# Four sequence mixers on one core: another rule for the order of the instructions, chains with buffers of their own, and transposes in a later step

## The chip, the cores and the metric

The kernel runs on one core of one Trainium2 chip. The metric is the device time of one execution in microseconds (us); lower is better. TensorE is called PE here, VectorE DVE, ScalarE ACT, GpSimd POOL and SyncE SP, as the profile does.

## The reference

The input x has 2048 tokens of 1024 features. One layer computes, in float32:

```python
h = _rmsnorm(x, pre_norm_w[l])
proj = jnp.einsum('btd,de->bte', h, w_in[l])
p_gdn, p_rwkv, p_sc, p_gla = _split(proj, [GDN_COLS, RWKV_COLS, SC_COLS, GLA_COLS])
...
y = jnp.concatenate([y_gdn, y_rwkv, y_sc, y_gla], axis=-1)
out = jnp.einsum('bte,ed->btd', y, w_out[l])
x = x + _rmsnorm(out, post_norm_w[l])
```

Each of the four mixers makes 256 of the 1024 features of y. Gated-delta (gdn) works in chunks of 64 tokens with 4 heads of 64: per chunk and head a lower triangular 64x64 matrix has to be inverted, and then a state of 64x64 goes from chunk to chunk:

```python
v_new = u_c - jnp.einsum('bhck,bhkv->bhcv', w_c, s)
o = jnp.einsum('bhck,bhkv->bhcv', q_c, s) + jnp.einsum('bhij,bhjv->bhiv', attn_c, v_new)
s = s * jnp.exp(gl_c)[..., None, None] + jnp.einsum('bhck,bhcv->bhkv', k_c, v_new)
```

RWKV-7 is written in the reference as one step per token; the kernel brings it into the same form (a triangular inverse per chunk and a state passed on). The short convolution (sc) has no state, and gated linear attention (gla) has a state but no inverse.

## The kernel before, in words

The 2048 tokens are cut into 4 blocks of 512 (`NBLK`, `BL`), a block into 4 tiles of 128 tokens (`TT`), a tile into 2 chunks. Per block there is much dense work on PE: the input projection, 760 matmuls of 512 columns that write the PSUM tiles called `pp` (`proj`, L476; each weight is used as a high and a low part, with the high and low part `hh`, `hl` of the normalised input). After the blocks the output projection has 768 more of them (`out_proj`, `woh` and `wol`), partly begun earlier; 3808 in all.

Beside it stand chains of small matmuls, which wait for DVE or ACT at nearly each step:

- the inverse (`inverse`, L558), once for two tiles, 16 times in all: steps on PE that write `psi`, eight matmuls each, in turn `psi<-X,Bb` (its result goes through DVE into `W`, L591) and `psi<-W,Yb` (through DVE into `X`, L596, and its transpose `Y`, L598, copied into `Yb`, L583);
- the chains of gdn (`gdn_chain`) and rwkv (`rwkv_chain`), in chunks one after the other: steps that write `psc`. One chunk of rwkv is `psc<-Sr,AR`, then an ACT copy into `ru` (L1034), `psc<-ru,Yf`, then DVE into `UV` (L1042), `psc<-UV,BKT`, then DVE into the state `Sr` (L1015);
- the preparation (`gdn_mats`, `rwkv_mats`, `gates_prep`, `rwkv_prep`), whose matmuls and transposes write `psa`.

What sets the order. First the program is recorded by generators (`chains`, `inverses`, `prepare`, `put`, `stats`, `projections`), which `weave` steps in turn on a clock of its own: it counts PE's time by the formulas in `mm` and `tr`, and a chain that yields a latency from the table `LAT` is taken up again when that much PE work has been recorded. `self.done` and a yielded tuple are events: ("B", n) is matrices n recorded, ("I", n) inverse n recorded, ("G", blk) and ("R", blk) the chain of a block. Then, when the `TileContext` closes (opened at L1431), its scheduler orders the recorded instructions of each engine by their priority and by its own clock of when operands, buffers and engines are ready, and puts in the semaphores. On the chip each engine takes its instructions in that order.

Buffers are rings (`RINGS`, `RINGS_G`, `RINGS16`): so many tiles of a name, used in turn. The part of the preparation for inverse n (`prepare`, L1110 on) waits for ("I", n - 1), since `Bh` and `Bl` have one buffer each.

Of the kernel before, what the change touches and what calls it, by code (L numbers as in the profile page):

```python
# [19 lines left out]
P = 128  # L20
# [105 lines left out]
class Ring:  # L126
# [6 lines left out]
    def __call__(self):  # L133
# [10 lines left out]

    "M4": (512, 4), "BKT": (512, 2), "UV": (512, 2), 
    "ru": (256, 2), "lu": (256, 3), "or": (256, 2),  "Yf": (64 * 8, 1), "y": (256, 1),
    "t2": (BL, 4), "gk": (16, 9), "sx": (64, 1), "dr": (16, 1), "kn": (4 * TT, 3), "rB": (256, 1), "sm": (16, 14),

# [5 lines left out]
RINGS_G = {  # L154
    "kq": (2 * BL, 2), "gv": (BL, 2), "ggz": (2 * BL, 1), "attn": (256, 2), "kT": (256, 4), "vT": (256, 2),
    "gu": (256, 3), "t1": (256, 3), "og": (256, 2), "gy": (256, 1),
}
RINGS16 = {"Bh": 1, "Bl": 1, "W": 1, "X": 2, "Y": 1}
RINGSBD = {"Bb": 1, "Yb": 2}
# [10 lines left out]

LAT = {"gates": 6.0, "ipre": 2.0, "gates2": 1.0, "norms": 3.2, "chan": 0.9, "pool": 1.38, "decay": 2.6, "mats": 2.2, "inv0": 1.0, "inv1": 2.2,
       "invr": 0.8, "chA": 1.0, "chB": 0.7, "chC": 0.48, "rpre": 5.0, "rchan": 4.5, "gpre": 3.0, "gA": 1.1,
# [15 lines left out]
class K:  # L188
# [581 lines left out]
    def gdn_mats(self, tt, Bh, Bl):  # L770
# [9 lines left out]
        nc.vector.tensor_tensor(h4(mb), m4(self.incl), bc(g["kb"]), ALU.mult)  # L780
        kT, vT = g["kT"][tt], self.R["vT"]()
        nc.vector.tensor_tensor(h4(kT), h4(kT), bc(g["ke"]), ALU.mult)
        ps = self.psa()
        for pr in range(2):
            self.tr(ps[:, pr * P:(pr + 1) * P], g["v"][pr][:, tt * P:(tt + 1) * P], self.ident)
        nc.vector.tensor_tensor(h4(vT), h4(ps[:, 0:256]), bc(g["kv"]), ALU.mult)
        yield LAT["pool"]
# [19 lines left out]
        nc.gpsimd.tensor_tensor(Bl, h4(B32), Bh, ALU.subtract)  # L807
        return dict(attn=h4(attn), kT=kT, vT=vT)

# [37 lines left out]
    def rwkv_prep(self, blk):  # L847
# [10 lines left out]
        for pr in range(2):  # L858
# [16 lines left out]
            ev = e.rearrange("p (a c) t -> p a c t", c=2)  # L875
            en, ak = self.t2(), self.t2()
            nc.scalar.activation(en, G, AF.Exp, scale=-1.0)
            kk = self.t2()
            nc.scalar.activation(m3(kk), k_, AF.Copy, scale=self.d[:, 23 + pr:24 + pr])
# [47 lines left out]
    def rwkv_mats(self, tt, Bh, Bl):  # L927
# [21 lines left out]
        nc.gpsimd.tensor_tensor(Bl, h4(B32), Bh, ALU.subtract)  # L949
        for pr in range(2):  # L950
            bd = BK[pr][:, 2 * tt:2 * tt + 2, :]
            for c in range(2):
                nc.scalar.activation(bd[:, c], bd[:, c], AF.Copy, scale=r["dec"][:, pr, 2 * tt + c:2 * tt + c + 1])
        yield LAT["rdec"]
        ps = self.psa()
        for cp in range(2):
            for pr in range(2):
                o = (2 * cp + pr) * P
                self.tr(ps[:, o:o + P], BK[pr][:, 2 * tt + cp, :], self.ident)
        bt = self.R["BKT"]()  # L960
        nc.scalar.copy(bt, ps)
        ps = self.psa()
# [3 lines left out]
        for cp in range(2):  # L966
            nc.scalar.copy(uv[hs(1 - cp), cp, :], ps[hs(cp), 0:256])
        return dict(M4=M4, bt=bt, uv=uv)

# [47 lines left out]
    def rwkv_chain(self, tt, m, Y):  # L1017
# [11 lines left out]
        for cp in range(2):  # L1029
# [80 lines left out]
    def prepare(self):  # L1110

        n = 0
        for blk in range(NBLK):
            for name in "GR":
                if name == "G":
                    yield "P", blk, "gdn"
                    yield from self.gates_prep()
                    yield from self.gdn_prep()
                else:
                    yield "P", blk, "rwkv"  # L1120
                    yield from self.rwkv_prep(blk)
                    self.done("Rprep", blk)
                for pair in range(TT // 2):
                    if n:
                        yield "I", n - 1
                    B, ms = [self.R16[x]() for x in ("Bh", "Bl")], []
                    for i in range(2):
                        if pair:
                            yield "T", name, blk, i
                        m = yield from (self.gdn_mats if name == "G" else self.rwkv_mats)(2 * pair + i, *(t[:, 4 * i:4 * i + 4, :] for t in B))  # L1130
                        ms.append(m)
                    self.mats[n] = ms, B
                    self.done("B", n, lat=LAT["mats"])
# [301 lines left out]
```

## Time and profile before

| | |
|---|---|
| time of 3 runs | 1380.93 us median (1374.62 to 1382.09) |
| profiled execution | 1382.66 us, span 1380.9 us |
| PE busy | 1286.0 us, 93% of the span |
| DVE, ACT, POOL busy | 966.9, 532.1 and 357.1 us |
| granted PE clock | 0.979 of full speed on average |
| DMA engines | 44.6% of their span |

A PE matmul's row covers its way through the array, so that rows that follow each other overlap; the pace is read from start to start. A row's bracket says how long the engine was idle before it, and what it waited for. DVE, ACT and POOL rows are the time of one instruction.

### The profile page before, as it was taken

To read this page: it belongs to the slowest core of one execution; us is meant where nothing else is said; L and a number is where in the kernel's file an instruction comes from. 1 tells how busy PE (TensorE), PEld (TensorE's weight loads), DVE (VectorE), ACT (ScalarE), POOL (GpSimd) and SP (SyncE) were. 2 spreads that over 40 slices of the span, in tenths; PEclk is the share of its full clock that TensorE was granted. 3 is DMA by queue.
4 is the path that set the end of the run, shared out by engine and by line. 5 is a ranking of instruction groups with operands and counts; after the bars stand their busy time and mean duration, and the time that the engine had idled before them with its cause. 6 is when DMAs were issued, how large, how long until landed. Compare 5 with 4: busy or idle time off the path is not lost. (4 is left out here: it accounts for less than half of the span.)

```text
span 1380.9 us, 25696 instructions
## 1 busy us (share of the span) xinstructions
PE 1286.0 (93%) x9928; PEld 974.5 (71%) x9928; DVE 966.9 (70%) x2194; ACT 532.1 (39%) x1165; POOL 357.1 (26%) x437
## 2 busy tenths in 40 slices
PE   5989988899999999999999899999998998999997
PEld 3767766667767777767677677676776776777886
DVE  5776697778886787688757894888669847643222
ACT  4653454235442441435524422453234234232221
POOL 5564443301121121111311211103112144232221
PEclk9999999999999999999999999999999998999999
DMA  7876554453244424453444333532444362233442
GB/s 278 272 253 228 206 176 145 142 167 121 92 139 136 155 93 151 140 177 123 139 145 137 123 126 130 165 125 93 146 134 142 117 213 87 93 111 100 150 151 99
DMA packets 98506, 204.47 MB, mean 148 GB/s; under 512 B 9152, under 2 KB 39248, under 8 KB 98384
## 3 DMA queue, kind: packets, MB, share of 16 engines
q1 hardware_dynamic: 98384, 202.83, 44.6%
q8 instruction: 78, 1.28, 0.4%
q14 instruction: 44, 0.36, 0.1%
HBM read 153.51 MB, written 49.28 MB: 147 GB/s over the span
## 5 line engine op out<-in xcount | busy, mean ns | idle before, releaser
L197 PE MATMUL pp<-hh,w 128*128 128x512 f32 (+1 forms) x2272 | 642.2, 408 | 7.9 <-ACT hh L432 4.0
L197 PEld LDWEIGHTS pp<-hh,w 128*128 128x128 f32 (+1 forms) x2272 | 413.0, 190 | 96.8 <-issue 5.1
L197 PE MATMUL pp<-hl,w 128*128 128x512 f32 (+1 forms) x1152 | 340.7, 408 | 2.0 <-POOL hl L433 2.0
L197 PEld LDWEIGHTS pp<-hl,w 128*128 128x128 f32 (+1 forms) x1152 | 209.3, 190 | 47.3 <-POOL hl L433 3.8
L350 POOL TENSOR_TENSOR w<-raw,w 128x512 fp32r<-128x512 f32 (+1 forms) x102 | 129.2, 1270 | 222.1 <-ACT w L349 121.6
L354 POOL TENSOR_TENSOR sm<-sm,mhalf 128x4 f32<-128x4 f32 (+1 forms) x64 | 59.7, 933 | 221.7 <-DVE sm L1077 196.0
L349 ACT CAST w<-raw 128x512 fp32r<-128x512 f32 (+1 forms) x102 | 60.4, 594 | 132.2 <-issue 60.9
L197 PE MATMUL pp<-woh,w 128*128 128x512 f32 x256 | 73.8, 409 | 0.0
L659 DVE SCALAR_TENSOR_TENSOR pq<-pq,par,pq 128x512 f32<-128x512 f32 x72 | 59.0, 819 | 14.7 <-ACT pq L656 12.3
L583 DVE COPY Yb<-Y 64x512 f16<-64x512 f16 x160 | 57.2, 358 | 2.2
L197 PEld LDWEIGHTS <-Yb 128*128 128x128 f16 x640 | 24.9, 99 | 44.5 <-issue 18.7
L197 PE MATMUL psi<-W,Yb 128*128 128x64 f16 x640 | 33.1, 196 | 23.5 <-DVE W L591 16.9
L197 PEld LDWEIGHTS pp<-woh,w 128*128 128x128 f32 x256 | 48.0, 193 | 9.5
L596 DVE TENSOR_TENSOR X<-psi,X 128x512 f16<-128x512 f32 x64 | 43.9, 686 | 9.6 <-PE psi L197 9.2
L197 PEld LDWEIGHTS <-Bb 128*128 128x128 f16 x768 | 29.6, 99 | 27.2 <-issue 21.6
L1368 DVE SCALAR_TENSOR_TENSOR pq<-pq,sm,x 128x512 f32<-128x512 f32 x32 | 24.0, 751 | 31.1 <-DMA x<-in_x 20.6
L598 DVE STREAM_TRANSPOSE Y<-X 128x512 f16<-128x512 f16 x64 | 45.2, 706 | 0.9
L1357 ACT ACTIVATE x<-pp 128x512 f32<-128x512 f32 x32 | 19.1, 598 | 68.8 <-PE pp L197 68.8
L591 DVE TENSOR_TENSOR W<-psi,c 128x512 f16<-128x512 f32 x64 | 43.6, 682 | 1.7 <-PE psi L197 1.2
L197 PE MATMUL psi<-X,Bb 128*128 128x64 f16 x768 | 39.7, 195 | 4.1 <-DVE X L596 3.6
L994 ACT COPY gu<-psc 64x128 f32<-64x128 f32 x64 | 16.7, 260 | 59.0 <-PE psc L197 58.0
L1358 DVE TENSOR_TENSOR pq<-pp,lg 128x512 f32<-128x512 f32 x16 | 11.1, 691 | 36.2 <-ACT x L1357 36.2
(317 smaller groups left out, 2087.2 us busy)
## 6 DMA issues: line engine op xcount, KB each, us to landing
w<-parts SPq DMA_DIRECT2D x186, 512.0 KB, 3.3
parts<-w SPq DMA_DIRECT2D x62, 512.0 KB, 4.0
raw<-in_wt SPq DMA_DIRECT2D x62, 256.0 KB, 3.1
x<-in_x SPq DMA_DIRECT2D x56, 256.0 KB, 3.0
raw<-yd SPq DMA_DIRECT2D x32, 256.0 KB, 2.9
out<-pq SPq DMA_DIRECT2D x32, 256.0 KB, 2.1
x<-in_xt SPq DMA_DIRECT2D x24, 256.0 KB, 2.9
yd<-y SPq DMA_DIRECT2D x32, 128.0 KB, 2.0
```

Source lines behind the costliest of these rows:

```text
L197: return self.nc.tensor.matmul(out, w, x, **kw)
L349: self.nc.scalar.copy(hi, src)
L350: self.nc.gpsimd.tensor_tensor(lo, src, hi.bitcast(F32), ALU.subtract)
L354: self.nc.gpsimd.tensor_tensor(dst, x, self.mhalf[:, 0:x.shape[1]], ALU.pow)
L583: nc.vector.tensor_copy(Yb[hs(c), :, hs(c)], Y[hs(c)])
L591: nc.vector.tensor_tensor(W, v(ps), m4(self.lev[lv]), ALU.mult)
L596: nc.vector.tensor_tensor(X2, v(ps), X, ALU.add)
L598: nc.vector.transpose(Y, X)
L659: nc.vector.scalar_tensor_tensor(acc, p[:, i:i + BL], self.pcol("conv", 4 * ct + i), acc, ALU.mult, ALU.add)
L994: nc.scalar.copy(qh(w)[q, :, hp, :], pB[hs(hp), 0:P].rearrange("p (q d) -> p q d", q=2))
L1357: nc.scalar.activation(junk, ps[i], AF.Square, accum_out=ss[:, i:i + 1])
L1368: nc.vector.scalar_tensor_tensor(o, o, r, x, ALU.mult, ALU.add)
```

## The change

- `TileContext` is opened with `schedule_with_timeline_sim=True`: the scheduler orders the same instructions by another model of time (a timeline model).
- `Bh` and `Bl` get two buffers instead of one, `M4` six instead of four, `attn` three instead of two. `prepare` waits for the inverse before the last, ("I", n - 2), not for the last.
- What the chains alone need, and the inverse doesn't, moves to a later step: `gdn_more` (the scaling of `kT`, the transposes of v, `vT`) and `rwkv_more` (the scaling of BK by the decay, its transposes and those of v). `chains` waits for it by a new event ("M", n).
- The transposed BK has no buffer `BKT` any more: it is written back into `BK`, with two ACT copies of 128x256 instead of one of 128x512.
- `t2` has three buffers instead of four (`kk` lives in `lw`, `ak` in `add`), and gdn's `gy` goes into `y`, which all three chains then share.

```diff
-    "M4": (512, 4), "BKT": (512, 2), "UV": (512, 2), 
+    "M4": (512, 6), "UV": (512, 2), 
...
-    "t2": (BL, 4), "gk": (16, 9), "sx": (64, 1), ...
+    "t2": (BL, 3), "gk": (16, 9), "sx": (64, 1), ...
...
-    "kq": (2 * BL, 2), "gv": (BL, 2), "ggz": (2 * BL, 1), "attn": (256, 2), ...
-    "gu": (256, 3), "t1": (256, 3), "og": (256, 2), "gy": (256, 1),
+    "kq": (2 * BL, 2), "gv": (BL, 2), "ggz": (2 * BL, 1), "attn": (256, 3), ...
+    "gu": (256, 3), "t1": (256, 3), "og": (256, 2),
...
-RINGS16 = {"Bh": 1, "Bl": 1, "W": 1, "X": 2, "Y": 1}
+RINGS16 = {"Bh": 2, "Bl": 2, "W": 1, "X": 2, "Y": 1}
...
+    def gdn_more(self, tt, m):
...
+        kT, vT = g["kT"][tt], self.R["vT"]()
+        nc.vector.tensor_tensor(h4(kT), h4(kT), bc(g["ke"]), ALU.mult)
+        ps = self.psa()
+        for pr in range(2):
+            self.tr(ps[:, pr * P:(pr + 1) * P], g["v"][pr][:, tt * P:(tt + 1) * P], self.ident)
+        nc.vector.tensor_tensor(h4(vT), h4(ps[:, 0:256]), bc(g["kv"]), ALU.mult)
+        m.update(kT=kT, vT=vT)
+        yield 0.0
...
-            en, ak = self.t2(), self.t2()
+            en, ak, kk = self.t2(), add[:, pr, :], lw
             nc.scalar.activation(en, G, AF.Exp, scale=-1.0)
-            kk = self.t2()
...
+    def rwkv_more(self, tt, m):
...
         yield LAT["rdec"]
         ps = self.psa()
-        for cp in range(2):
-            for pr in range(2):
-                o = (2 * cp + pr) * P
-                self.tr(ps[:, o:o + P], BK[pr][:, 2 * tt + cp, :], self.ident)
-        bt = self.R["BKT"]()
-        nc.scalar.copy(bt, ps)
+        for pr, bd in enumerate(bds):
+            for cp in range(2):
+                o = (2 * pr + cp) * P
+                self.tr(ps[:, o:o + P], bd[:, cp], self.ident)
+        for pr, bd in enumerate(bds):
+            nc.scalar.copy(bd, ps[:, 2 * P * pr:2 * P * pr + 2 * P].rearrange("p (c x) -> p c x", c=2))
...
-        y = self.R["gy"]()
+        y = self.R["y"]()
...
-                    if n:
-                        yield "I", n - 1
+
+                    if n > 1:
+                        yield "I", n - 2
...
+                    self.done("B", n, lat=LAT["mats"])
                     for i in range(2):
                         if pair:
                             yield "T", name, blk, i
...
+                        yield from more(2 * pair + i, ms[i])
+                    self.done("M", n, lat=LAT["more"])
                     n += 1
...
                         yield "I", n
+                        yield "M", n
...
-    with tile.TileContext(nc) as tc:
+    with tile.TileContext(nc, schedule_with_timeline_sim=True) as tc:
```

How the instructions stand. First PE late in the second block's projection, before: from the end of one step of the inverse to the start of the next one.

```order
L197 LDWEIGHTS Yb_153
L197 MATMUL psi<-W_147,Yb_153 128x64
L197 MATMUL pp<-hh,w_159 128x512 x4
L197 MATMUL pp<-hl,w_159 128x512 x4
L197 LDWEIGHTS Bb_151
L197 MATMUL psi<-X_148,Bb_151 128x64
```

The same place on PE, now.

```order
L197 LDWEIGHTS Bb_152
L197 MATMUL psi<-X_150,Bb_152 128x64
L197 MATMUL pp<-hh,w_161 128x512 x4
L197 MATMUL pp<-hh,w_159 128x512 x4
L197 MATMUL pp<-hl,w_159 128x512 x4
L197 MATMUL pp<-hh,w_159 128x512 x4
L197 MATMUL pp<-hh,w_160 128x512 x4
L197 MATMUL pp<-hl,w_160 128x512 x2
L197 LDWEIGHTS Yb_154
L197 MATMUL psi<-W_148,Yb_154 128x64
```

Between two steps of the inverse stood 8 projection matmuls, and now stand 22. Over the whole program the 3808 projection matmuls are broken up by small ones 434 times before (229 of the pieces are exactly 8 long) and 253 times now (113 of the pieces are 15 to 24 long).

Second, PE in the last block's rwkv chain, just ahead of the first output projection matmuls, before: from one step `psc<-ru,Yf` (the ACT copy `ru` by the inverse) to the next but one.

```order
L197 MATMUL psc<-ru_80,Yf_87 64x64 x4
L197 MATMUL pp<-hl,w_160 128x512 x4
L197 MATMUL pp<-hh,w_160 128x512 x4
L197 MATMUL psc<-UV_78,BKT_76 64x64 x4
L197 MATMUL pp<-hh,w_158 128x512 x2
L197 MATMUL pp<-hl,w_158 128x512 x2
L197 MATMUL pp<-hh,w_158 128x512 x2
L197 MATMUL pp<-hh,w_159 128x512 x2
L197 MATMUL psc<-Sr,AR_63 128x128
L197 MATMUL psc<-Sr,AR_64 128x128
L197 MATMUL pp<-hl,w_159 128x512 x2
```

The same steps on PE, now.

```order
L197 MATMUL psc<-ru_80,Yf_87 64x64 x4
L197 MATMUL psc<-UV_78,BK_65 64x64 x2
L197 MATMUL psc<-UV_78,BK_66 64x64 x2
L197 MATMUL psc<-Sr,AR_63 128x128
L197 MATMUL psc<-Sr,AR_64 128x128
L197 MATMUL psc<-ru_80,Yf_87 64x64 x4
L197 MATMUL psc<-UV_78,M_72 64x64 x2
L197 MATMUL psc<-UV_78,M_73 64x64
L197 MATMUL psc<-UV_78,BK_65 64x64 x2
L197 MATMUL psc<-UV_78,BK_66 64x64 x2
```

Where 8 projection matmuls stood between two dependent steps, none stands now. The first of these rows belongs to a stretch of 512 small matmuls without any projection matmul, at the end of the fourth block (after 3040 of 3808); the longest such stretch before has 78.

## Rows read from the trace of the kernel before

**Rows 1.** The page's busy times, with shares of the span and instructions.

```profile
PE 1286.0 (93%) x9928; PEld 974.5 (71%) x9928; DVE 966.9 (70%) x2194; ACT 532.1 (39%) x1165; POOL 357.1 (26%) x437
```

**Rows 2.** Busy time of each engine in chosen stretches.

```profile
core 0: us, PE busy (x) PEld busy (x) DVE busy (x) ACT busy (x) POOL busy (x), PEclk, DMA share, GB/s
0.00:25.00 25.00, 9.89 (x34) 6.41 (x35) 13.35 (x37) 11.80 (x25) 14.14 (x20) 1.00 0.85 298
175.00:200.00 25.00, 20.11 (x115) 15.08 (x113) 23.25 (x33) 13.84 (x23) 12.34 (x10) 0.86 0.45 167
225.00:250.00 25.00, 19.83 (x156) 15.27 (x155) 21.11 (x44) 11.05 (x29) 8.68 (x8) 0.94 0.47 157
600.00:650.00 50.00, 50.00 (x414) 38.05 (x412) 44.72 (x106) 23.07 (x49) 4.18 (x12) 1.00 0.42 136
```

**Rows 3.** Who waited for whom on PE: total us, times, longest.

```profile
PE psi L197 <- DVE W L591: 16.9, 11, 4.8
PE psa L201 <- POOL gs L354: 12.1, 1, 12.1
```

**Rows 4.** Projection matmuls by operands: busy us, mean ns, idle before.

```profile
L197 PE MATMUL pp<-hh,w 128*128 128x512 f32 (+1 forms) x2272 | 642.2, 408 | 7.9 <-ACT hh L432 4.0 <-DMA w<-parts 2.4 <-ACT BK L953 1.5
L197 PE MATMUL pp<-hl,w 128*128 128x512 f32 (+1 forms) x1152 | 340.7, 408 | 2.0 <-POOL hl L433 2.0
L197 PE MATMUL pp<-woh,w 128*128 128x512 f32 x256 | 73.8, 409 | 0.0
L197 PE MATMUL pp<-wol,w 128*128 128x512 f32 x128 | 35.1, 394 | 0.0
```

**Rows 5.** PE in order of time, output projection: start us, us, what.

```profile
1282.56 1.07 PE L197 MATMUL pp<-woh,w 128*128 128x512 f32 x4
1283.47 1.07 PE L197 MATMUL pp<-hh,w 128*128 128x512 f32 x4
```

**Rows 6.** PE and DVE in order of time, an inverse beside the projection.

```profile
601.59 0.41 PE L197 MATMUL psi<-X,Bb 128*128 128x64 f16 x8
601.83 1.17 PE L197 MATMUL pp<-hl,w 128*128 128x512 f32 x4
...
602.80 0.69 DVE L591 TENSOR_TENSOR W<-psi,c 128x512 f16<-128x512 f32 x1
602.84 1.08 PE L197 MATMUL pp<-hh,w 128*128 128x512 f32 x4
...
603.76 0.41 PE L197 MATMUL psi<-W,Yb 128*128 128x64 f16 x8
...
604.21 0.69 DVE L596 TENSOR_TENSOR X<-psi,X 128x512 f16<-128x512 f32 x1
...
607.08 1.17 PE L197 MATMUL pp<-hh,w 128*128 128x512 f32 x4
...
608.09 1.08 PE L197 MATMUL pp<-hl,w 128*128 128x512 f32 x4
...
609.02 0.41 PE L197 MATMUL psi<-W,Yb 128*128 128x64 f16 x8
```

**Rows 7.** PE and DVE in order of time, around PE's longest such wait.

```profile
187.50 0.68 DVE L591 TENSOR_TENSOR W<-psi,c 128x512 f16<-128x512 f32 x1
...
188.24 0.58 PE L197 MATMUL psi<-W,Yb 128*128 128x64 f16 x8 [4.79 <-DVE W L591]
...
188.63 1.20 PE L197 MATMUL pp<-hh,w 128*128 128x512 f32 x2
188.86 0.69 DVE L596 TENSOR_TENSOR X<-psi,X 128x512 f16<-128x512 f32 x1 [0.42 <-PE psi L197]
```

**Rows 8.** ACT instructions that the edits touch or resemble, by line.

```profile
L961 ACT COPY BKT<-psa 128x512 f32<-128x512 f32 x16 | 9.3, 584 | 5.0 <-PE psa L201 4.9
L1289 ACT COPY lu<-psc 128x256 f32<-128x256 f32 x16 | 6.0, 373 | 16.2 <-issue 9.5 <-DVE Sl L1281 4.6 <-PE psa L201 1.4
L552 ACT ACT_TABLE_LOAD x4 | 5.1, 1283 | 0.1
```

More of the change, by code (lines that the diff above doesn't have):

```diff
@@ L143 @@
     "rv": (BL, 2), "rgz": (2 * BL, 1), "radd": (2 * BL, 1), "E1": (NC * 65, 1),
-    "M4": (512, 4), "BKT": (512, 2), "UV": (512, 2),
+    "M4": (512, 6), "UV": (512, 2),
     "ru": (256, 2), "lu": (256, 3), "or": (256, 2),  "Yf": (64 * 8, 1), "y": (256, 1),
-    "t2": (BL, 4), "gk": (16, 9), "sx": (64, 1), "dr": (16, 1), "kn": (4 * TT, 3), "rB": (256, 1), "sm": (16, 14),
+    "t2": (BL, 3), "gk": (16, 9), "sx": (64, 1), "dr": (16, 1), "kn": (4 * TT, 3), "rB": (256, 1), "sm": (16, 14),
     "lqk": (BL, 2), "lv": (BL, 2), "lkv": (384, 1), "lgz": (2 * BL, 1), "ld": (8, 1), "lg": (BL, 2), "n32": (32, 4), "gs": (TT, 2),
@@ L154 @@
 RINGS_G = {
-    "kq": (2 * BL, 2), "gv": (BL, 2), "ggz": (2 * BL, 1), "attn": (256, 2), "kT": (256, 4), "vT": (256, 2),
-    "gu": (256, 3), "t1": (256, 3), "og": (256, 2), "gy": (256, 1),
+    "kq": (2 * BL, 2), "gv": (BL, 2), "ggz": (2 * BL, 1), "attn": (256, 3), "kT": (256, 4), "vT": (256, 2),
+    "gu": (256, 3), "t1": (256, 3), "og": (256, 2),
 }
-RINGS16 = {"Bh": 1, "Bl": 1, "W": 1, "X": 2, "Y": 1}
+RINGS16 = {"Bh": 2, "Bl": 2, "W": 1, "X": 2, "Y": 1}
 RINGSBD = {"Bb": 1, "Yb": 2}
@@ L169 @@
 BANKS = {"pp": 2, "psa": 3, "psi": 1, "psc": 2}
-LAT = {"gates": 6.0, "ipre": 2.0, "gates2": 1.0, "norms": 3.2, "chan": 0.9, "pool": 1.38, "decay": 2.6, "mats": 2.2, "inv0": 1.0, "inv1": 2.2,
+LAT = {"gates": 6.0, "ipre": 2.0, "gates2": 1.0, "norms": 3.2, "chan": 0.9, "pool": 1.38, "decay": 2.6, "mats": 2.2, "more": 1.4, "inv0": 1.0, "inv1": 2.2,
        "invr": 0.8, "chA": 1.0, "chB": 0.7, "chC": 0.48, "rpre": 5.0, "rchan": 4.5, "gpre": 3.0, "gA": 1.1,
@@ L780, in gdn_mats @@
         nc.vector.tensor_tensor(h4(mb), m4(self.incl), bc(g["kb"]), ALU.mult)
-        kT, vT = g["kT"][tt], self.R["vT"]()
-        nc.vector.tensor_tensor(h4(kT), h4(kT), bc(g["ke"]), ALU.mult)
-        ps = self.psa()
-        for pr in range(2):
-            self.tr(ps[:, pr * P:(pr + 1) * P], g["v"][pr][:, tt * P:(tt + 1) * P], self.ident)
-        nc.vector.tensor_tensor(h4(vT), h4(ps[:, 0:256]), bc(g["kv"]), ALU.mult)
         yield LAT["pool"]
@@ L807, in gdn_mats @@
         nc.gpsimd.tensor_tensor(Bl, h4(B32), Bh, ALU.subtract)
-        return dict(attn=h4(attn), kT=kT, vT=vT)
+        return dict(attn=h4(attn))
+    def gdn_more(self, tt, m):
+        nc = self.nc
+        g = self.g
+        bc = lambda s: s[:, 4 * tt:4 * tt + 4].unsqueeze(2).to_broadcast([P, 4, 64])
+        kT, vT = g["kT"][tt], self.R["vT"]()
[6 more added lines that the diff above has]
+        yield 0.0
     def rwkv_proj(self):
@@ L949, in rwkv_mats @@
         nc.gpsimd.tensor_tensor(Bl, h4(B32), Bh, ALU.subtract)
-        for pr in range(2):
-            bd = BK[pr][:, 2 * tt:2 * tt + 2, :]
+        yield 0.0
+        return dict(M4=M4)
+    def rwkv_more(self, tt, m):
+        nc = self.nc
+        r = self.r
+        BK = r["BK"]
+        bds = [BK[pr][:, 2 * tt:2 * tt + 2, :] for pr in range(2)]
+        for pr, bd in enumerate(bds):
             for c in range(2):
@@ L955, in rwkv_mats @@
         ps = self.psa()
-        for cp in range(2):
-            for pr in range(2):
-                o = (2 * cp + pr) * P
-                self.tr(ps[:, o:o + P], BK[pr][:, 2 * tt + cp, :], self.ident)
-        bt = self.R["BKT"]()
-        nc.scalar.copy(bt, ps)
+        for pr, bd in enumerate(bds):
+            for cp in range(2):
+                o = (2 * pr + cp) * P
+                self.tr(ps[:, o:o + P], bd[:, cp], self.ident)
+        for pr, bd in enumerate(bds):
+            nc.scalar.copy(bd, ps[:, 2 * P * pr:2 * P * pr + 2 * P].rearrange("p (c x) -> p c x", c=2))
         ps = self.psa()
@@ L967, in rwkv_mats @@
             nc.scalar.copy(uv[hs(1 - cp), cp, :], ps[hs(cp), 0:256])
-        return dict(M4=M4, bt=bt, uv=uv)
+        m.update(bt=bds, uv=uv)
     def gdn_chain(self, tt, m, Y):
@@ L1046, in rwkv_chain @@
             for h in range(4):
-                o = (2 * cp + h // 2) * P + 64 * (h % 2)
-                self.mm(pC[hs(h % 2), hs(h // 2)], bt[:, o:o + 64], uv[:, cp, hs(h)], start=True, stop=True)
+                self.mm(pC[hs(h % 2), hs(h // 2)], bt[h // 2][:, cp, hs(h % 2)], uv[:, cp, hs(h)], start=True, stop=True)
             self.add_state(S, pC)
@@ L1123, in prepare @@
                 for pair in range(TT // 2):
-                    if n:
-                        yield "I", n - 1
+                    if n > 1:
+                        yield "I", n - 2
                     B, ms = [self.R16[x]() for x in ("Bh", "Bl")], []
+                    mats, more = (self.gdn_mats, self.gdn_more) if name == "G" else (self.rwkv_mats, self.rwkv_more)
+                    for i in range(2):
+                        tt = 2 * pair + i
+                        if tt == 3:
+                            yield "T", name, blk, 0
+                        m = yield from mats(tt, *(t[:, 4 * i:4 * i + 4, :] for t in B))
+                        ms.append(m)
+                    self.mats[n] = ms, B
+                    self.done("B", n, lat=LAT["mats"])
                     for i in range(2):
@@ L1129, in prepare @@
                             yield "T", name, blk, i
[L1130 to L1133, printed above, removed]
+                        yield from more(2 * pair + i, ms[i])
+                    self.done("M", n, lat=LAT["more"])
                     n += 1
```

## The prediction

> **What bounds the kernel now.** I read the busy times first. PE is busy in 1286.0 of 1380.9 us, DVE in 966.9 [rows 1], so PE bounds the kernel and 94.9 us of it are idle. A busy PE could still be a slow one, so I looked for its pace: in the output projection four 512-column matmuls start every 0.907 us, 0.227 us each [rows 5]. There are 2272 + 1152 + 256 + 128 = 3808 of them [rows 4], which makes 863.7 us at that pace. The rest of PE's busy time, 422 us, goes to 4372 small matmuls (8180 stand in the order) and to the breaks between the two kinds.
>
> A break has a price: between two inverse steps, 8 projection matmuls begin at 607.08 and the next step at 609.02, 1.94 us where 8 x 0.227 = 1.81 [rows 6]. That is 0.13 us, and 434 breaks make 56 us. So a small matmul costs (422.3 - 56) / 4372 = 0.084 us on average.
>
> Then the stretches in time. Of the first 25 us PE works 9.9, and 12.1 us of that wait is one wait for the statistics [rows 2, 3]. In a good stretch, 600 to 650 us, PE is busy in 50.00 of 50 us while DVE works for 44.7 [rows 2]: the chains run entirely under the projection. The reader can see how in the order of time [rows 6]: a `psi` step at 601.59, four projection matmuls, DVE's W at 602.80, the next step at 603.76, DVE's X at 604.21. Eight projection matmuls (1.8 us) are just about the time that a step needs to go to DVE and back. Where they aren't enough, PE waits: 16.9 us in 11 waits for W alone [rows 3]. The worst shows the way in which both engines take their work: PE stands still for 4.79 us before `psi<-W,Yb`, although projection matmuls stand right behind it [rows 7].
>
> So the kernel's time is PE's work plus what is not covered, and what covers a chain step is the projection matmuls that stand in the order just there. The order is what the change alters most.
>
> **The change part by part: the small edits.** The number of matmuls of each kind stays, and DVE has the same work. `BKT`'s 16 copies of 0.584 us become 32 of half the width; the nearest row is 0.373 us, so ACT gets 2.6 us more [rows 8]. The built program has 15 loads of an activation table where it had 9: 6 x 1.283 = 7.7 us of ACT [rows 8]. ACT is busy for 532 of 1381 us [rows 1] and hides both where PE has other work; at worst all 10 us are seen. `y` now serves three chains, one `t2` less is there, and both add waits of DVE, which the order shows but not what they cost; doubled `Bh`, `Bl` and the later step let the matrices for the next inverse be made early, and take waits away. I count all of this together as 0, with 10 us either way.
>
> **The order.** The projection is cut into 253 pieces instead of 434. That removes 181 breaks, 24 us. In the stretches that stay covered, about 20 matmuls (4.5 us) stand between dependent steps that needed about 2, so nearly all of the present waits go: of 94.9 - 15.1 = 79.8 us outside the start I keep 10.
>
> But each of the 16 inverses has some 14 steps in a row, and each tile two rounds of its chain. At 22 projection matmuls a step, a block's 760 don't reach: they run out while the chains are half done. The order shows where. Before the next projection matmul there stand 21 groups of small matmuls after 760 of the 3808, and 51, 58, 41, 58, 37, 94 and 19 groups after 1064, 1520, 1824, 2280, 2584, 3040 and 3232: eight bare stretches of 1976 small matmuls, with 86 inverse steps and 164 groups of the chains, many of them waiting for the group before. In the order before, no stretch has more than 11 groups.
>
> What a bare stretch takes is set by DVE. I counted the DVE instructions between the first that needs a PE result from within the stretch and the last that PE waits for in it: 742 in the eight (177 of the inverse, 216 of the chains, 76 of the norms, about 130 of rwkv's preparation, the rest smaller). They can't have run earlier, and DVE takes them in order. At DVE's mean of 966.9 / 2194 = 0.441 us [rows 1] they are 327 us if DVE never waits. That is the floor. The ceiling is no overlap at all: from the end of W at 188.18 to the start of X at 188.86 a step's way over PE costs 0.68 us [rows 7], and 86 inverse steps and about 120 dependent chain steps make 206 x 0.68 = 140 us on top, 467 us; with the hops over ACT and POOL about 500 us, DVE busy in 65%. In the two stretches of before in which PE waits most, DVE is busy in 93% (175 to 200 us) and 84% (225 to 250) [rows 2]. The second is full of gated-delta's chain and is the nearer case, so I take 85%: 327 / 0.85 = 385 us.
>
> **The clock.** After its long waits PE's granted clock falls: 0.86 of full speed in the mean of 175 to 200 us [rows 2], and the eight-matmul step at 188.24 takes 0.58 us where those of rows 6 take 0.41 [rows 6, 7]. With the bare stretches PE works in under half of the time there, so I expect the lower level, 1.2 GHz, in much of them. If all 206 dependent steps were slowed by 0.17 us that would be 35 us; if none, 0. I take 15, since the 85% already has some of it. The Trainium skill, "TensorE: Matmul & The Clock Gate", section "What's actually happening", says that the slow clock is PE's default and that only activity lifts it. By that rule the whole of the bare stretches would run slow, and the sum would come out at the 35 us end. The row agrees as far as one long wait goes.
>
> **The sum.** Outside the bare stretches PE has 863.7 us of projection, 253 breaks at 0.13 = 33 us, and 4372 - 1976 = 2396 small matmuls at 0.084 = 201 us: 1097 us. The bare stretches take 385, the start 15, remaining waits 10, the clock 15: 1522 us of span. The profiled execution is 1.8 us longer than its span, 1382.66 us, and 0.1% over the median of the runs, so the two can be compared as they are: 1524, say 1525 us, 10% more than before.
>
> The floor is 1097 + 327 + 15 + 2 = 1441 us, less at most 10 for the small edits. The ceiling is 1097 + 500 + 15 + 10 + 35 + 2 = 1659.
>
> The Trainium skill, "Perfetto Trace Analysis", section "Optimization Strategy", advises to interleave regimes that have different contended engines. It speaks against this order, which pulls the two apart; 600 to 650 us shows what the interleaving is worth here, 50 us of PE and 44.7 of DVE in 50.
>
> **The rivals.** (a) The bare stretches are a chain without overlap, DVE below 65%: over 1640 us, about 1680. For it: in the last rwkv rounds each DVE instruction needs the PE result of the one or two before. Against it: in most stretches an inverse, a chain and a preparation run side by side.
>
> (b) It gets faster. The waits go (70 us), the breaks go (24 us), and the chains' tails are short because the matrices are made ahead: 1383 - 94 = 1289 if the bare stretches cost no more than their own PE work (1976 x 0.084 = 166 us). For it: the doubled buffers do what this needs. Against it: the 742 DVE instructions follow PE results inside the stretches and so can't be made ahead. The point from which it decides: all eight together under 1381 - 1097 - 27 = 257 us, 70 us below DVE's floor.
>
> (c) The order doesn't matter, since PE would take later projection matmuls while it waits: about 1380, or 10 us around it. The 4.79 us wait with projection matmuls behind it [rows 7] speaks against it.
>
> (d) Half of it: DVE's share of a stretch starts before PE's piece ahead of it ends. With 4.5 us per stretch that is 36 us off my sum, still inside the range; only with much larger leads would the time be 1390 to 1435.
>
> **How the numbers follow.** My forecast, bare stretches bound by DVE, has 0.80, with its own range 1441 to 1640. (a) has 0.10, (b) 0.05, (c) 0.02, (d) as far as it leads under 1435, 0.03. A measurement of this kernel can tell about 0.5%, 7 us, from no change. Slower is then 0.80 + 0.10 + 0.03 = 0.93, faster 0.05, the same 0.02. The range for 8 in 10 is 1435 to 1640: it leaves out (a) to (c) and the low end of (d).
>
> **What would show it.** In the busy tenths of the page, PE must fall to 3 to 6 where the bare stretches are: at the four block ends, at 40% of the second, third and fourth block, and once in the output projection, the longest (about 100 us) at the end of the fourth block, with DVE at 8 or 9 in the same slices. PE's idle time must rise from 95 to some 250 us or more, mostly waits for DVE's W, X, gu, UV and Sr, while the waits for W between long pieces of projection are gone. PE's busy time should fall by 24 us or so. The clock should show under 9 in the bare slices. I am wrong if PE stays over 90% busy, or if the new idle time is at the projection's own weights or PSUM tiles (a DMA or an evacuation that comes late), not at the chains; and the mechanism is right with a wrong size if the bare stretches are there, but DVE is far from 85% in them.

## Result and the profile after

The changed kernel takes 1593.38 us (median of 4 runs, 1588.39 to 1595.54) against 1379.53 of the kernel before on the same chip: a ratio of 1.155 (95% interval 1.1506 to 1.1593). The forecast was 1525 us, range 1435 to 1640. The profiled execution has a span of 1593.7 us, 72 us over the sum of 1522.

The page's busy times of the changed kernel answer to [rows 1]:

```profile
PE 1397.3 (88%) x9928; PEld 1083.6 (68%) x9928; DVE 974.5 (61%) x2194; ACT 546.0 (34%) x1187; POOL 350.2 (22%) x437
```

DVE has the same work (966.9 before, 974.5 now). PE has the same matmuls and is nevertheless busy for 111 us longer; its idle time went from 95 to 196 us. The page's busy tenths, 40 slices of 39.8 us, show where:

```profile
PE   6999998897899967997999867996999857989998
DVE  4775688746545499655454699566453796743322
PEclk9999997997799957996899858996999655988999
```

PE and its clock fall together at slices 15 and 16, 24 and 25, and 32 to 34, with DVE at 9 in the first two places and at 7, 9 and 6 in the third. These are the ends of the second, third and fourth block's projection. The bare stretches were then located in the trace, from the last projection matmul before each to the first after it. These are their windows, in the columns of [rows 2]: start and end, length, busy time of each engine with its instructions, PE's clock, DMA.

```profile
core 0: us, PE busy (x) PEld busy (x) DVE busy (x) ACT busy (x) POOL busy (x), PEclk, DMA share, GB/s
241.10:263.80 22.70, 19.82 (x159) 15.68 (x157) 20.91 (x47) 15.69 (x39) 7.07 (x7) 0.68 0.08 26
369.80:418.30 48.50, 32.45 (x375) 24.32 (x373) 32.36 (x83) 20.09 (x48) 4.12 (x7) 0.59 0.16 50
550.80:618.20 67.40, 42.39 (x399) 33.00 (x398) 62.83 (x147) 31.49 (x71) 11.04 (x9) 0.64 0.03 9
724.90:764.00 39.10, 28.10 (x328) 20.85 (x327) 23.29 (x64) 12.04 (x29) 3.70 (x5) 0.57 0.11 36
898.00:965.70 67.70, 43.24 (x408) 33.83 (x407) 63.85 (x149) 31.60 (x72) 11.38 (x10) 0.62 0.03 11
1077.30:1114.80 37.50, 24.97 (x285) 18.65 (x284) 23.12 (x59) 13.47 (x27) 2.33 (x5) 0.61 0.08 25
1246.10:1357.30 111.20, 74.18 (x705) 58.49 (x704) 93.59 (x222) 45.88 (x104) 29.96 (x25) 0.56 0.11 35
1412.70:1431.90 19.20, 13.51 (x159) 9.89 (x158) 11.49 (x32) 3.53 (x10) 3.52 (x4) 0.64 0.12 38
sum 413.30, PE 278.64 PEld 214.71 DVE 331.46 ACT 173.80 POOL 73.12; mean PE 34.83 PEld 26.84 DVE 41.43 ACT 21.72 POOL 9.14
```

All eight are there, where the order showed them, 413.3 us together. (The rows count more than the order's 1976 small matmuls, since most float32 ones of the chains stand twice in the trace: `psc<-ru,Yf` is x4 in the order and x8 here.) A ninth stretch, of 10.6 us after projection matmul 3280, is not in the sum. The reader should divide DVE's busy time by the length of each row. Four stretches are full of DVE: 92, 93, 94 and 84% (at 241, 551, 898 and 1246). Four are not: 67, 60, 62 and 60%. In the latter PE is busy for 67 to 72%, so neither engine is full. In three of them the last inverse ends early, and its end cuts the row in two. Here is the second stretch up to there and behind it, and what is left behind it of the fourth and the sixth:

```profile
369.80:387.50 17.70, 10.15 (x179) 8.03 (x177) 15.25 (x37) 2.62 (x7) 1.74 (x2) 0.75 0.12 38
387.50:418.30 30.80, 22.30 (x196) 16.29 (x196) 17.11 (x47) 17.47 (x41) 2.38 (x5) 0.50 0.19 56
...
736.00:764.00 28.00, 21.82 (x219) 15.81 (x218) 13.66 (x42) 9.79 (x23) 1.93 (x3) 0.50 0.08 25
...
1085.00:1114.80 29.80, 21.58 (x212) 16.04 (x210) 17.57 (x49) 13.47 (x27) 2.33 (x5) 0.56 0.02 6
```

Beside the inverse DVE is busy for 86% of the second stretch (87 and 72% in the heads of the other two, 11.1 and 7.7 us long). In the three tails, 88.6 us together, it is at 56, 49 and 59%, PE at 72 to 78%, and PE's clock is 0.50 to 0.56, which is 1.2 GHz nearly throughout. PE's `psc` steps are 32, 40 and 39% of the chain that ended last there; most of that work is rwkv's. These are three of its steps, in order of time (start, us, what, and the wait before):

```profile
388.26 0.69 PE L197 MATMUL psc<-ru,Yf 64*64 64x64 f32 x8 [0.88 <-DVE Yf L636]
389.63 0.70 PE L197 MATMUL psc<-UV,BK 128*64 128x64 f32 x8 [0.68 <-DVE UV L1057]
391.01 1.22 PE L197 MATMUL psc<-Sr,AR 128*128 128x128 f32 x4 [0.69 <-DVE Sr L1030]
```

Each step waits for the one before on another engine, and each is slow. The same steps in the kernel before, between pieces of projection (of three chunks' rows the three kinds):

```profile
302.69 0.71 PE L197 MATMUL psc<-Sr,AR 128*128 128x128 f32 x4
...
305.98 0.45 PE L197 MATMUL psc<-ru,Yf 64*64 64x64 f32 x8
...
309.43 0.45 PE L197 MATMUL psc<-UV,BKT 128*64 128x64 f32 x8 [0.71 <-DVE UV L1042]
```

Some of PE's longest waits in the whole span (total us, times, longest), to compare with [rows 3]:

```profile
PE psc L197 <- DVE gu L999: 20.0, 15, 2.7
PE psa L201 <- ACT E L882: 15.5, 2, 8.0
...
PE psc L197 <- DVE UV L1057: 11.4, 11, 2.9
PE psa L197 <- DVE AR L895: 11.0, 3, 3.9
PE psi L197 <- DVE Yb L583: 10.9, 10, 2.3
PE pp L197 <- ACT hh L432: 10.0, 8, 2.4
...
PE psc L197 <- DVE Sr L1030: 7.3, 9, 1.7
...
PE psi L197 <- DVE W L591: 1.2, 2, 0.8
```

and before, of the chains' steps:

```profile
PE psc L197 <- DVE gu L984: 8.1, 11, 2.9
...
PE psc L197 <- DVE UV L1042: 3.1, 5, 0.8
```

The wait for `W` (L591), 16.9 us before, has nearly gone, and those of the chains' steps (`gu`, `UV`, `Sr`) have grown. New are two waits for `E` and three for `AR`, steps of rwkv's preparation on ACT and DVE; they lie inside the bare stretches at 551, 898 and 1246 us, beside a DVE that is busy for 84 to 94%. The wait for `hh` is no chain's. It stands where a block begins, right behind a bare stretch:

```profile
263.80:313.80 50.00, 40.46 (x287) 28.62 (x285) 42.64 (x94) 12.98 (x25) 4.44 (x9) 0.87 0.44 140
618.20:668.20 50.00, 42.56 (x326) 30.85 (x327) 38.75 (x86) 14.22 (x30) 4.37 (x8) 0.87 0.39 124
965.70:1015.70 50.00, 40.89 (x314) 28.84 (x316) 38.45 (x86) 13.07 (x28) 3.39 (x7) 0.86 0.34 111
```

There PE is idle for 9.5, 7.4 and 9.1 us more. The longest wait in the first of these windows, then the longest in the third:

```profile
PE pp L197 <- ACT hh L432: 3.8, 2, 2.4
```

```profile
PE psi L197 <- DVE W L604: 2.8, 1, 2.8
```

All waits of the three windows sorted by what they are for (a wait that begins before its window counts whole): 11.6 us for `hh` and `hl`, the next block's normalised input, 13.4 us for steps of the inverses and chains, and 3.7 us for weights and `pq`.

### The profile page after: what moved, and what is told of

The parts are those of the page before. It is cut to its first block, busy times and chain, and to the rows that moved or that the text cites. A ratio compares the mean times of both kernels' runs of the same rounds, so it can differ in the third digit from the quotient of the medians.

```text
span 1593.7 us, 25725 instructions
## 1 busy us (share of the span) xinstructions
PE 1397.3 (88%) x9928; PEld 1083.6 (68%) x9928; DVE 974.5 (61%) x2194; ACT 546.0 (34%) x1187; POOL 350.2 (22%) x437
## 4 chain that ended last, share of the span: by engine, by line
PE 66%; DVE 21%; issue 4%; ACT 4%; DMA 3%; POOL 2%; SPq 0%; ACTq 0%; POOLq 0%; DVEq 0%
PE pp L197 50%; PE psc L197 8%; PE psa L197 4%; PE psi L197 3%; PE psa L201 2%; DVE Y L598 1%; DVE x L426 1%; DVE Yb L583 1%; DVE W L591 1%; DVE M L949 1%; DVE X L596 1%; DVE pq L659 1%; DMA raw<-in_wo 1%; POOL sm L354 1%; DVE gu L1000 1%
## 5 line engine op out<-in xcount | busy, mean ns | idle before, releaser
L197 PE MATMUL pp<-hh,w 128*128 128x512 f32 (+1 forms) x2272 | 625.0, 404 | 14.7 <-ACT hh L432 10.0
L197 PEld LDWEIGHTS pp<-hh,w 128*128 128x128 f32 (+1 forms) x2272 | 421.6, 191 | 109.2 <-ACT hh L432 11.5
L197 PEld LDWEIGHTS pp<-hl,w 128*128 128x128 f32 (+1 forms) x1152 | 214.9, 190 | 54.0 <-DVE hl L433 7.1
L596 DVE TENSOR_TENSOR X<-psi,X 128x512 f16<-128x512 f32 x64 | 44.0, 688 | 49.0 <-PE psi L197 48.2
L197 PE MATMUL psa<-AR,BK 64*128 64x128 f32 x256 | 45.0, 368 | 18.5 <-DVE AR L895 11.0
L591 DVE TENSOR_TENSOR W<-psi,c 128x512 f16<-128x512 f32 x64 | 43.8, 684 | 28.3 <-PE psi L197 27.4
L197 PEld LDWEIGHTS <-Bb 128*128 128x128 f16 x768 | 34.5, 105 | 34.6 <-issue 31.4
L197 PEld LDWEIGHTS psa<-AR,BK 64*128 64x128 f32 x256 | 38.0, 258 | 23.2 <-DVE AR L895 11.4
L197 PE MATMUL psi<-W,Yb 128*128 128x64 f16 x640 | 37.5, 208 | 16.7 <-DVE Yb L583 10.9
L583 DVE COPY Yb<-Y 64x512 f16<-64x512 f16 x160 | 48.7, 304 | 2.0
L197 PE MATMUL psc<-UV,M 128*64 128x64 f32 (+1 forms) x512 | 38.8, 274 | 6.1 <-DVE UV L1057 5.1
L197 PEld LDWEIGHTS psc<-UV,M 128*64 128x64 f32 (+1 forms) x512 | 29.8, 177 | 17.1 <-DVE UV L1057 6.5
```

Of the source, the lines that this page charges most:

```text
L197: return self.nc.tensor.matmul(out, w, x, **kw)
L583: nc.vector.tensor_copy(Yb[hs(c), :, hs(c)], Y[hs(c)])
L591: nc.vector.tensor_tensor(W, v(ps), m4(self.lev[lv]), ALU.mult)
L596: nc.vector.tensor_tensor(X2, v(ps), X, ALU.add)
```

## The experiments

Theory: the projection runs ahead of the chains that it should cover, and what is left bare costs what DVE and the way between the engines take. Rivals: the edits cost the time; DVE's or ACT's order does; PE's low clock does. Ratios are to the kernel before, run on the same chip.

**Edits without the new order.** The changed kernel with `tile.TileContext(nc)` as before.

> The changed kernel without the flag: the doubled buffers, the later steps, BKT in BK and the shared y stay, the scheduler orders with its usual model. Theory (the loss of 214 us lies in the order that the timeline model gives PE): no bare stretch is left in PE's order (the longest run of groups without a projection matmul has 10), so 1360 to 1395 us. Rival (the edits carry the loss: stores of the shared y, the write-back into BK, fewer t2): 1480 to 1600 us.

1389.39 us, ratio 1.0098 (1.007 to 1.0127). No bare stretch; the edits alone cost 1%.

**The new order without the edits.**

```diff
-    with tile.TileContext(nc) as tc:
+    with tile.TileContext(nc, schedule_with_timeline_sim=True) as tc:
```

> The kernel before with the flag alone. Theory (order): twelve bare stretches with 801 DVE instructions of the kind counted for the changed kernel, which had 742 in 413 us; 801 x 413 / 742 = 446 us, so 33 us over the changed kernel, about 1625 (1570 to 1680). Rival (the edits carry it): 1370 to 1400 us.

1600.97 us, ratio 1.1616 (1.1559 to 1.1673). The stretches after all its long pieces add up to some 440 us (446 by the forecast), DVE busy in 82%; here are the first and the longest.

```profile
228.70:261.50 32.80, 18.25 (x157) 13.53 (x155) 31.11 (x62) 15.15 (x29) 6.25 (x6) 0.58 0.06 21
1262.40:1363.40 101.00, 62.50 (x602) 49.10 (x601) 80.46 (x183) 38.44 (x82) 24.50 (x20) 0.54 0.10 31
```

So the loss comes with the flag, that is, with another order of the same instructions, whatever the edits are. The whole is 24 us under the 1625 forecast, inside its range.

**PE in the recorded order, with and without the timeline model.** Every matmul and transpose keeps the place in which it was recorded; the model then orders only the other engines.

```diff
-        return self.nc.tensor.matmul(out, w, x, **kw)
+        return self.tc.keep_in_program_order(self.nc.tensor.matmul(out, w, x, **kw))
...
-        return self.nc.tensor.transpose(out, x, ident)
+        return self.tc.keep_in_program_order(self.nc.tensor.transpose(out, x, ident))
```

> The changed kernel with the flag, but every matmul and transpose pinned behind the one recorded before it: PE runs in the order that the kernel's own weave recorded, and only DVE, ACT, POOL and the queues are ordered by the timeline model. Theory (PE's order alone): no bare stretch of ten or more groups, so 1360 to 1410 us. Rival (the timeline model's order of DVE and ACT costs as well or instead: chain work stands behind evacuations there): 1450 us or more, with PE waiting for DVE at many places outside any bare stretch.

> As e3, PE in the recorded order, but without the flag, so that DVE, ACT and POOL are ordered by the usual model. PE's order is word for word that of e3. Theory: within 1.5% of e3 and of e1 (1355 to 1410 us). Rival of e3 (order of DVE and ACT matters): 1360 to 1400 here and 1450 or more in e3.

1431.04 us, ratio 1.0385 (1.0343 to 1.0427), and without the model 1431.98 us, 1.0394 (1.0347 to 1.0441). PE's order is the same in both. With PE in this order, DVE's and ACT's order by the model therefore costs nothing; no run has the model's order on PE alone. It only moves the waits here; the first two of each run's largest on chains are

```profile
PE psc L197 <- DVE gu L999: 41.8, 20, 5.6
PE psi L197 <- DVE Yb L583: 24.3, 8, 7.0
```

with the model and

```profile
PE psi L197 <- DVE W L591: 41.8, 24, 5.4
PE psc L197 <- DVE gu L999: 23.6, 20, 4.8
```

without. My ranges for both were some 20 us too low: the recorded order itself is 42 us worse than what the old scheduler makes of it (1389, the edits alone).

**Only the projection in its recorded place.**

```diff
-        return self.nc.tensor.matmul(out, w, x, **kw)
+        i = self.nc.tensor.matmul(out, w, x, **kw)
+        return self.tc.keep_in_program_order(i) if n == BL and (w.dtype == F32R) else i
```

> The changed kernel with its flag, in which only the 512-column projection matmuls keep their recorded place on PE, behind the small ones that were recorded before them; the small matmuls are still ordered by the timeline model, but can't be left behind the projection. The longest stretch without a projection matmul has 13 to 17 groups. Theory (projection matmuls taken ahead of the chains that they should cover are the loss): no bare stretch, 1380 to 1430 us (the order with every matmul in its recorded place took 1431). Rival (the model's order of the small matmuls and of the chains among themselves is also bad): over 1500 us, with waits for DVE's W, gu and UV spread over the blocks.

1482.25 us, ratio 1.0762 (1.0728 to 1.0797): between the two forecasts. Keeping the projection back takes 111 of the 214 us away, about half. Another 51 us go when the small matmuls keep their places too (1431). The theory named only the first part. In this run the longest time without projection is

```profile
850.50:868.80 18.30, 12.96 (x107) 10.31 (x106) 17.04 (x40) 10.02 (x27) 5.02 (x6) 0.67 0.12 43
```

and PE is busy for 1325.0 us against 1285.5 with all in place, idle for 152.9 against 146.0. So the 51 us are mostly PE's busy time, of which the time at the lower clock (149 against 112 us) explains at most 18. The rest is open.

**Longer and shorter pieces, with the old scheduler.** If the length of the pieces is the cause, the kernel before must suffer from it too. `BEAT` sets how long its own weave stays with the projection.

```diff
-BEAT = 1.5
+BEAT = 3.4
```

> The kernel before, with its own scheduler, but BEAT = 3.4 instead of 1.5: its weave takes up longer pieces of projection between two steps of a chain. In its order one long bare stretch stands after projection matmul 3040 (66 groups, 315 small matmuls, about 120 DVE instructions) and a short one after 760 (18 groups, 38 DVE instructions); the other blocks have none. Theory (a bare stretch costs its DVE instructions, at the 413 us for 742 of them in the changed kernel = 0.557 us each): 67 us and 21 us of bare stretch at 3.4 GFLOP-free PE work, so some 88 - 353 x 0.084 = 58 us more than they would take covered, less up to 20 us of breaks saved: 1400 to 1430 us. Rival (it is the timeline model, not the length of the pieces): 1370 to 1390 us.

1417.05 us, ratio 1.0285 (1.0257 to 1.0314). The two stretches were forecast at 21 and 67 us:

```profile
225.70:252.70 27.00, 10.97 (x90) 7.43 (x89) 26.62 (x51) 14.86 (x24) 5.98 (x6) 0.59 0.07 22
1131.00:1197.40 66.40, 48.91 (x467) 38.73 (x465) 47.99 (x116) 22.02 (x56) 20.15 (x18) 0.53 0.14 43
```

With 51 and 116 DVE instructions that is 0.53 and 0.57 us each; the forecast had 0.557. (The 3.4 in the expectation is the value of `BEAT` and no rate of work.) The whole lies inside its forecast. So a bare stretch costs about the same per DVE instruction without the timeline model and without the edits. Then the other way, shorter pieces:

```diff
-BEAT = 1.5
+BEAT = 0.8
```

> The kernel before, with BEAT = 0.8 instead of 1.5: shorter pieces of projection, 498 breaks between projection and small matmuls instead of 434, the longest stretch without projection 13 groups. Theory (more breaks at 0.13 us each, 8 us more, and pieces shorter than a step's way to DVE and back, so more waits for W): 1385 to 1400 us. Rival (shorter pieces take the chains up earlier and end the waits): under 1372 us.

1390.85 us, ratio 1.0102 (1.0074 to 1.0129): too short costs as well, 1%. The reason forecast for it isn't seen: PE waits less for `W` than before, where it was 16.9 us [rows 3].

```profile
PE psi L197 <- DVE W L591: 10.3, 8, 2.7
```

What the 1% consists of stays open.

**What sets the length of a bare stretch: more work for PE, or more for DVE.** Both change only the inverses 13 and 14, which stand in the longest stretch.

```diff
+EXTRA = 6
...
+            if n in (13, 14):
+                spare = self.psa()
+                for u in range(EXTRA):
+                    self.nc.tensor.matmul(v(spare), l[:, u, :], r, start=True, stop=True)
```

> The changed kernel with six more 512-column float16 matmuls, into a PSUM tile that nobody reads, behind each W or X step of the inverses 13 and 14, which stand mostly in the bare stretch after projection matmul 3040 (111.2 us, PE 74.2 busy, clock 0.56, in the changed kernel). Theory (DVE, and the way there and back, set this stretch's length): it is 110 to 125 us long though PE works more, the whole 1590 to 1610 us, ratio to the changed kernel 1.00 to 1.01. Rival (the low clock of PE sets it): the clock in it rises to over 0.8, and it is 85 to 97 us long, the whole 1570 to 1580 us.

```diff
+        def extra(t):
+            if n in (13, 14):
+                for u in (0, 1, 2, 4, 5):
+                    nc.vector.tensor_tensor(self.Z, t[:, u:u + 3, :], I16[:, 0:3, :], ALU.add)
...
+            extra(W)
...
+            extra(X2)
```

> The changed kernel with five more DVE instructions of 128x192 (f16, nobody reads their result) behind each W and X of the inverses 13 and 14: 80 in all, mostly in the bare stretch after projection matmul 3040, whose order on PE stays as it is (111.2 us, DVE busy in 93.6 of them, 17.6 idle, in the changed kernel). Their duration is not known; from the 128x512 f16 ones (0.43 to 0.52 us) I put it at 0.2 us, 16 us together. Theory (DVE's own work sets the length of a bare stretch): the stretch grows by nearly all of what these instructions are busy, 12 to 18 us, the whole 1605 to 1612 us, ratio to before 1.163 to 1.170. Rival (the way from engine to engine sets it, and DVE's 17.6 idle us take them up): the stretch grows by 0 to 5 us, the whole 1593 to 1598 us.

With the spare matmuls 1605.19 us, ratio 1.1655 (1.1621 to 1.169); with the spare DVE work 1604.23 us, 1.165 (1.1625 to 1.1675). The stretch, first with the matmuls, then with the DVE work:

```profile
1240.70:1374.20 133.50, 93.83 (x901) 62.39 (x900) 109.52 (x248) 46.59 (x109) 34.32 (x29) 0.74 0.11 33
```

```profile
1242.90:1367.40 124.50, 76.87 (x706) 61.25 (x705) 108.60 (x302) 45.89 (x104) 31.26 (x26) 0.53 0.11 31
```

The 80 DVE instructions are busy for 20.9 us:

```profile
L579 DVE TENSOR_TENSOR Z<-X,c 128x192 f16<-128x192 f16 x40 | 11.0, 275 | 0.5
L579 DVE TENSOR_TENSOR Z<-W,c 128x192 f16<-128x192 f16 x40 | 9.9, 248 | 0.5
```

All 80 lie in the stretch, beside the 222 instructions that were there. DVE's busy time rose by only 15.0 us, since its rows overlap by some 5 us more than they did, and the stretch grew by 13.3. Of the 17.6 us in which DVE had been idle only 1.7 were used up. So DVE's work does set the length of this stretch, as forecast; the whole kernel's 1604 is just under the forecast of 1605 to 1612. One reservation: some of the 80 stand in DVE's order right ahead of the next step of the same inverse, where they would also lengthen a chain that leaves DVE idle; the run doesn't part the two.

The spare matmuls, 120 in all, raised the clock from 0.56 to 0.74, short of the 0.8 that the rival had named, and the stretch got longer, not shorter. It got longer than the theory said too: with the new order 26 more DVE instructions and 76 more small matmuls came into it; DVE's share is 82%, against 84%. This run doesn't tell what a higher clock would give by itself, because the spare matmuls take PE's time and a `psa` tile as well.

**Which of the edits cost the 1%.** The edits without the flag, and with the old condition for the preparation.

```diff
-                    if n > 1:
-                        yield "I", n - 2
+                    if n:
+                        yield "I", n - 1
```

> The edits without the flag (1389 us, 1.0 percent over before), but with the preparation waiting for the last inverse again, not for the one before the last. Theory (the preparation that is let ahead takes DVE's time before the W and X that PE waits for): 1373 to 1380 us, ratio to before 0.995 to 1.003, and PE's wait for W back from 20.9 to about 17 us. Rival (the later steps and the shared buffers cost the 1 percent): 1386 to 1392 us, ratio 1.007 to 1.012.

1372.92 us, ratio 0.9962 (0.9938 to 0.9987). So the run-ahead costs the 1%, and the rest of the edits gains 0.4% (0.1 to 0.6). The reason that I had given fell, though. PE's wait for `W` without the run-ahead, ahead of that with it (first this run, then the edits alone):

```profile
PE psi L197 <- DVE W L591: 20.1, 17, 4.1
```

```profile
PE psi L197 <- DVE W L591: 20.9, 18, 2.9
```

It is no shorter. PE is busy for 1273.5 instead of 1288.5 us and at the lower clock for 23 instead of 53 us, in one profile each, and this run's is of an execution of 1367 us, 6 under its median. What links that to the run-ahead is open.

**Less work for DVE in a covered order.** The copies `Yb<-Y` go to ACT, first on top of the run before, then on the kernel before.

```diff
-                nc.vector.tensor_copy(Yb[hs(c), :, hs(c)], Y[hs(c)])
+                nc.scalar.copy(Yb[hs(c), :, hs(c)], Y[hs(c)])
```

> The edits without the flag and without the run-ahead (1373 us, 0.9962 of before), with the 160 copies Yb<-Y (57 us of DVE) on ACT, which is busy in 39 percent. Theory (PE's waits in a covered order are for DVE's W, 20 us, which comes late because DVE is full): PE's waits for W and X fall by 5 to 15 us, 1358 to 1368 us. Rival (the copy takes longer on ACT, and behind other ACT work, and PE now waits for Yb instead, 3.0 us before): 1370 to 1385 us, waits for Yb over 10 us.

> The kernel before, with the 160 copies Yb<-Y on ACT and nothing else changed. In the edits without flag and run-ahead the same move took 1372.9 to 1359.1 us, a ratio of 0.9907. Theory (the gain is DVE's 57 us, and doesn't hang on the edits): 1361 to 1370 us, ratio 0.988 to 0.994, PE's waits for W from 16.9 to 4 to 8 us. Rival (it needs the room that the later steps leave on DVE and ACT ahead of an inverse): 1374 to 1382 us, ratio 0.997 to 1.003.

1359.05 us, ratio 0.9869 (0.9846 to 0.9893), the fastest kernel of this study, and 1366.23 us, 0.9919 (0.9894 to 0.9945). A copy takes longer on ACT, 616 ns against 358 on DVE before (first the kernel before, then the faster kernel):

```profile
L583 DVE COPY Yb<-Y 64x512 f16<-64x512 f16 x160 | 57.2, 358 | 2.2
```

```profile
L583 ACT COPY Yb<-Y 64x512 f16<-64x512 f16 x160 | 98.5, 616 | 75.4 <-DVE Y L598 66.7 <-DVE Y L577 5.6 <-DVE sm L1084 1.6
```

But it comes off the engine that `W` and `X` wait for. PE's waits in the faster kernel, where those for `W` and `Yb` were 20.1 and 3.0 us (that for `X`, L596, rose from 2.8 to 5.5):

```profile
PE psi L197 <- ACT Yb L583: 5.8, 6, 2.9
PE psi L197 <- DVE W L591: 4.3, 6, 1.2
```

and in the kernel before with the copies moved, where that for `W` was 16.9 [rows 3]:

```profile
PE psi L197 <- DVE W L591: 3.7, 4, 2.2
```

Both times lie in the ranges forecast. In the kernel before, that wait is not all of it: with the copies moved, PE's idle time fell by 8.4 us and its busy time by 7.9, in one profile each; why the busy time fell is open.

## Why the prediction was right in kind and 72 us short

**The step that decides was right.** Which stretches are bare was read from the order, and the run has these eight, and beside them only one short one. The four experiments on the order (flag alone, all of PE in place, projection in place, longer pieces) put the loss there: on the order of PE, about half of it on the projection that runs ahead, and with PE in its recorded place none on DVE's or ACT's order. Rival (c), that the order doesn't matter, is refuted by the flag alone, and (b) by the sum of the stretches, 413 us where it needed under 257. Rival (d), a lead of DVE, isn't seen: the windows hold more DVE instructions than were counted, not fewer.

**The bare stretches: 413.3 us against 385.** The floor came out right, 327 us against 331.5 us of DVE in the windows, and in part by luck: the windows hold 803 DVE instructions at 0.413 us, where 742 at 0.441 were counted. The step that failed is the share, one 85% taken for all from the nearest window of before. It measured 331.5 / 413.3 = 80%, and this mean hides two kinds. In the four stretches with inverses and chains side by side, DVE had 241.2 of 269.0 us, 90%, better than I had put it. In the four after projection matmuls 1064, 1824, 2584 and 3232 (at 370, 725, 1077 and 1413 us), where in most of the time only a chain is left, it had 90.3 of 144.3 us, 63%; at 85% they would have been 106 us, so that 38 us were lost here, of which the full ones gave 15 back (the 85% would have made them 284 us); the other 5 are the floor's. There rival (a) is right in kind, which I had weighed over all stretches at once. The order could have told three of them apart: the last `psi` step comes early there, `psc` and `psa` steps go on alone, and little is left to fill DVE.

**The clock.** I had put 15 us on top. The mean over the eight windows, weighted by their lengths, is 0.602 of full speed, so 80% of their time is at 1.2 GHz and the rest at 2.4. The Trainium skill, "TensorE: Matmul & The Clock Gate", section "What's actually happening", makes the slow clock the default that only activity lifts. The trace agrees as to the level; the 35 us that I had drawn from it are not reached by the estimate below. My premise that PE works in under half of the time there was wrong: it is busy for 278.6 of 413.3 us, 67%, and the level is the lower one all the same. PE's busy time shows it: I had forecast a fall by 24 us, and it rose by 111. The bare stretches' matmuls, at the mean of before 1976 x 0.084 = 166 us, are busy for 278.6. Not all of that need be the clock, since the row of a step that nothing follows counts whole, while under the projection the next row began 0.24 us after the start of a row of 0.41 [rows 6]. In the DVE-bound longest stretch the spare matmuls gave no sign that the low clock costs time. In the three tails I think it does: PE has 36, 66 and 62% of the chain that ended last there, 48 us, and its steps take 0.69 or 0.70 us for 0.45, or 1.22 for 0.71. At the ratio 0.45 / 0.69 that is 17 us, at one half 24 us, so that the 15 were of the right size; but they are a part of the low share above and no term beside it. This is an estimate from the rows; no run raised the clock in a tail.

**Outside: 1180.4 us against 1122.** PE is busy there for 1397.3 - 278.6 = 1118.7 us; I had 1097. The lower clock accounts for at most 8 of the 22 us, since it lasts for 76 us outside the stretches, against 61 in all before; the rest I put down to my averages for a small matmul and a break, which no run tests. PE is idle for 61.7 us instead of 25. The first 25 us have 14.7 of it, where I had 15. The term that failed is the 10 us of remaining waits: it measured 47. What I left out is the start of each block, 26 us in the three windows shown. There PE comes back to a projection whose `hh` and `hl` aren't ready, for at most 11.6 us; and steps of the inverses and chains, which I had taken to be covered again as soon as the projection goes on, are waited for about as long, 13.4 us. The rest is spread. At the weights and PSUM tiles, where I had looked for a sign of being wrong, there are about 4 us.

The four add up: 28.3 + 21.6 + 36.7 - 15 = 72 us. Two of my signs failed with them: PE's idle time is 196 us and not 250, because PE is busy for 278.6 us of the bare stretches where I had 166, and its tenths fall to 5 to 7, not 3 to 6; at 40% of the blocks DVE stands at 5 or 6, not at 8 or 9.

**The small edits: 0 by my count, with 10 us either way; +13 us by the edits alone** (0.7 to 1.3%). Doubled `Bh` and `Bl` were to take waits away. The early preparation that they allow costs about 19 us with the old scheduler (ratios 1.0098 against 0.9962), and the rest of the edits gains about 5. Under the new order the runs show no cost of the edits (1.155 with them, 1.1616 without; the intervals overlap).

The Trainium skill, "Perfetto Trace Analysis", section "Optimization Strategy", advises to interleave regimes with different contended engines. The runs agree with it on one side only: the longer pieces of `BEAT` = 3.4 cost 1.0285, but the shorter ones of 0.8, which interleave more, cost 1.0102.

## What to carry to other kernels

Where dense matmuls cover chains that go over other engines, count in the order how many dependent steps stand between two pieces of dense work: a bare stretch cost its DVE work divided by 0.9 here where an inverse and chains ran side by side in it, and by 0.5 to 0.6 where one chain was left. A scheduler that lets dense work run ahead can take the cover away from the chains that needed it; keep the dense work in its recorded place and look again (that gave back 111 of 214 us here), and look at what the other engines owe to the next dense stage. In a covered order, move work off the engine that the chain waits for, even to one that takes longer for it (616 ns for 358 gained 0.8 to 0.9% here).

## Unexpected of the hardware

- PE's busy share is no measure of its work when the clock and the order change: the same matmuls were busy for 111 us more, at a mean clock of 0.874 instead of 0.979.
- A PE that is busy for three quarters of a stretch with short dependent matmuls still runs it mostly at 1.2 GHz (72 to 78% busy, clock 0.50 to 0.56 in the tails); in the longest stretch 120 matmuls of 512 columns in between lifted the clock from 0.56 only to 0.74.
